# Layer 0 of a two-layer attention backbone: filling products queued behind the score product of three tiles back, and the output projection divided anew over four groups of steps

## The chip, the cores and the metric

The kernel runs on one core of a Trainium2 chip. The metric is the device time of one execution in microseconds, as the median of three runs. A profile of one further execution goes with it. Its engines are named as in the profile: PE is the matrix engine (PEld its loading of the stationary operand), DVE the vector engine, ACT the scalar engine, POOL the general engine, SP the engine that issues most DMA transfers. Each engine works through its own list of instructions in order.

## The reference

Two layers over 1024 latent tokens with a prefix of 256 context tokens, width 1024. The change lies in layer 0, the even layer:

```python
h = rms_norm(x, norm_g[0]) * (1 + scale) + shift          # latent and context tokens
aq, ak, av, ag, bq, bk, bv, bg = split_cols(h @ w_in, EVEN_WIDTHS)
# A: 8 heads on 2 key/value heads, all 1280 keys, RMS norm and rotary on q and k
# B: 8 heads on 2 key/value heads, context keys and a window of +-128, rotary, a sink logit
oa = softmax(q k^T / 8) v ;  ob = the same with window mask and sink
y = concatenate([oa * silu(ag), ob * silu(bg)]) @ w_out
x = x + gate * y                                          # then layer 1, final rms_norm
```

Layer 1 (a convolution module and a neighbourhood attention) follows and isn't touched. Its first step needs the normed rows of layer 0's result.

## The kernel before

All products are made from values split into a high and a low part (`split`, line 310), three matrix products for each (`mm3`, lines 327 to 329): high by high, low by high, high by low. The tokens are cut into chunk 0 (256 context tokens) and chunks 1 and 2 (512 latent tokens each).

**Units.** Layer 0's attention is done in four units, one for each key/value head, in the order 2, 3, 0, 1. Units 2 and 3 are windowed (branch B), units 0 and 1 are global (branch A). A unit has ten blocks of 128 queries, and a block has two to ten tiles of 128 keys: 42 tiles in a windowed unit, 84 in a global one. In this document the tiles of layer 0 are counted through from 0: 0 to 41 and 42 to 83 are the windowed units, 84 to 167 and 168 to 251 the global ones.

**A tile** (`attn_gen`): the score product `st` (line 491, with 495, and 494 for a mask), the exponential on ACT (line 503), the split into `ph` and `pl` (ACT, then POOL or DVE), and three products `ov` (lines 447 to 449) three tiles later. For each block there are also products for the maxima of its scores (`mx`, lines 602, 614, 622), whose results DVE reduces, and a small transpose `trn` (line 425) that puts the maxima into `QL`, which the second half of the score product reads.

**Fill.** Between the tiles stand products of other work: the projection of the next unit (`pq`, `proj_qkv`, 240 products of 384 columns), its gate (`pg`, `proj_gate`, 144 products), and the output projection (`po`, `out0`), in three parts by the units whose results it needs: `out0_part(parts[0])` for the first two units (288 products), `out0_part(parts[1])` for the third (144) and `final_proj` for the fourth (48 for each chunk). `norm_h` makes layer 1's input from a finished chunk. The tails of the projection (`qk_tail`, transposes `trk` at line 858) also stand there. A unit's keys and values lie in one of two buffers in turn.

**What sets the order.** `weave` runs a number of steps of the attention (two for each tile) and draws steps of fill at an even rate between them; `later(FL[0])` gives the fill a lower rank by 80. The finished program's order isn't that of the code: a scheduler takes, for each engine, what is ready by its own reckoning, the attention first by rank. Fill that is ready can so be placed long ahead of the step that drew it. `weave` has an argument `lag`: where it isn't 0, each product of fill is given an edge to the score product that stands `lag` places from the end of the list of those drawn so far (`sts`), and must come behind it in PE's list. Before, layer 1 uses it and layer 0 doesn't.

**Numbers.** `N0` are the steps that the gate's rest is spread over, `NLAST` the steps at a unit's end for which no fill is drawn, `NFILL` the steps of fill drawn between. `O1` are the steps for the output projection in the last unit, by groups: reading back the units' results (`load_oh`), part one, part two, and the share of the final work (`final_proj(1)`, `norm_h(1)`, `final_proj(0)`, `norm_h(0)`) that is drawn before the attention ends. `final_proj(2)` and `norm_h(2)` come behind it all.

Of the kernel before, what the change touches and what calls it, by code (L numbers as in the profile page):

```python
# [67 lines left out]
NFILL = (39, 39, 36)  # L68
GL = 12
HV = 'gggvvvvg'  # L70
O1 = (6, 65, 41, 14)
TICK0, TICK1 = (1, 3)
PLAN = 'p0mmnbwmm1h2nbhnbh'
MWR = "ABxAVx"
# [13 lines left out]
def tile_kernel(ctx: ExitStack, tc: tile.TileContext, a, out):  # L88
# [435 lines left out]
    def weave(main, nmain, fill, nfill, last=True, all_fill=True, lag=0):  # L524

        done = 0
        for k in range(nmain):
            next(main, None)
            while done * nmain < (k + 1) * nfill:
                with ExitStack() as cx:  # L530
                    cx.enter_context(later(FL[layer[0]]))
                    if lag and len(sts) >= lag:
                        cx.enter_context(tc.issue_after(sts[-lag].ins))
                    next(fill, None)
                done += 1
        if all_fill:
            for _ in fill:
                pass
        if last:
            for _ in main:  # L540
                pass
# [131 lines left out]
    with ExitStack() as p0x:  # L673
# [111 lines left out]
        def proj_gate(u, ms):  # L785

            if u not in gw:
                gw[u] = load_g0(u) if u == ORDER[0] else load_w0("ev_g", u)
            wh, wl = gw[u]
            for m, c in ms:  # L790
                t0, n = CHUNKS[c]
                pp = bank("pp", nm("pg"))
                for dk in range(DK):
                    ms_ = slice(m * P, (m + 1) * P)
                    mm3(pp[:, :n], wh[dk][:, ms_], wl[dk][:, ms_], Hs(h, 0, t0, n, dk), Hs(h, 1, t0, n, dk),
                        dk == 0, dk == DK - 1)
                    if dk % 3 == 1:
                        tick()
                        yield
                sg = ap.tile([P, 640], F32, tag="rt2", name=nm("sg"), bufs=2)  # L800
                silu2(pp[:, :n], sg[:, :n])
                mark[0] = SY.dma_start(Gs[u][:, m, t0 : t0 + n], sg[:, :n])
                for _ in range(2):
                    if tails:
                        qk_tail(*tails.pop(0))
# [61 lines left out]
        def gblocks(k):  # L867

            if k == 3:
                blocks = [(m, c) for c in range(3) for m in range(2)]  # L870
                return blocks[:GB], blocks[GB:]
            return [(0, c) for c in range(3)], [(1, c) for c in range(3)]

        def fill0(k, w=None):
            yield from proj_qkv(ORDER[k], w)
            yield from proj_gate(ORDER[k], gblocks(k)[0])
# [4 lines left out]
        main = attn_gen(a0, [group0(u, qb) for u in ORDER for qb in QORD], VS0, LOOK0)  # L881
        for k in range(4):
            u = ORDER[k]
            n = NSTEP[u // 2] + (12 if k == 0 else 0)
            if k < 3:
                n0 = N0[1 + u // 2] if k else N0[0]
                n1 = n - n0 - NLAST[u // 2]
                weave(main, n0, proj_gate(u, gblocks(k)[1]), 9, False)
                weave(main, n1, fill0(k + 1), NFILL[k], False)
                weave(main, NLAST[u // 2], iter(()), 0, False)  # L890
            else:
                weave(main, GL, proj_gate(u, gblocks(k)[1]), 18 - 3 * GB, False)
# [4 lines left out]
    with tc.tile_pool(name="o0", bufs=1, reuse_waits="tile") as op_:  # L897
        U1 = ORDER[-1]
        parts = [[2 * u + k for u in sorted(us) for k in range(2)] for us in (ORDER[:2], ORDER[2:3], ORDER[3:])]
        final = parts[2]  # L900
        x1 = []
        def load_oh(fs):

            f0, f1 = fs[0], fs[-1] + 1
            for c in range(3):
                t0, n = CHUNKS[c]
                if fs == parts[0]:
                    oh[c] = new_h(c)
                    x1.append(op_.tile([P, DK, n], F32, tag=f"x1_{c}", name=nm("x1"), bufs=1))
                for f in range(f0, f1, 2):  # L910
                    lo = oh[c][1][:, f : f + 2, :]
                    (SY, SC)[OHQ].dma_start(lo.bitcast(F32), Od[:, f : f + 2, t0 : t0 + n])
                    split(lo.bitcast(F32), oh[c][0][:, f : f + 2, :], lo, "s", OHE)
                    yield
# [21 lines left out]
        def out0_part(fs):  # L936
            for e2 in range(4):
                w = load_w(op_, a["ev_wo"], e2, 256, WO, dks=fs, rb=2)
                if fs == parts[0]:
                    load_x1(e2)  # L940
                for e in (2 * e2, 2 * e2 + 1):
                    for c in range(3):
                        yield from out0(fs, e, c, *w)
# [30 lines left out]
            yield  # L974

        weave(main, O1[0], load_oh(parts[0]), 6, False)
        weave(main, O1[1], out0_part(parts[0]), 48, False)
        weave(main, O1[2], chain(load_oh(parts[1]), out0_part(parts[1])), 30, False)
        ws = [load_w(op_, a["ev_wo"], e2, 256, WO, "gv"[e2 % 2], dks=final, rb=2) for e2 in range(4)]
        fill = chain(final_proj(1), norm_h(1), final_proj(0), norm_h(0))  # L980
        weave(main, NSTEP[U1 // 2] - GL - O1[0] - O1[1] - O1[2], fill, O1[3])
# [612 lines left out]
```

## Time and profile before

| | |
|---|---|
| three runs, median (lowest to highest) | 1579.01 us (1578.08 to 1581.34) |
| the profiled execution | 1581.59 us |
| its span, first to last instruction | 1579.8 us, 21684 instructions |
| mean clock granted to PE | 0.962 |
| layer 0's attention, first to last score product | 133.0 to 926.5 us |
| windowed units | to 502 us |
| global units | 502 to 926.5 us |

The share of the span is given for each engine; matrix products overlap in the pipeline, so that their busy times are longer than the distance at which they start. Where a row of the trace names a wait, it is the idle time of the engine ahead of an instruction, with what ended it. A row "by stretches" gives a stretch of the span in us, its length, then for each engine busy time and number of instructions, the granted clock, the DMA engines' mean busy share and the rate in GB/s; asked for one line or tile it counts those instructions alone.

### The profile page before, as it was taken

The page shows a single profiled execution, that of the slowest core. Times are in us where ns is not written, and L with a number is a line of the kernel's source. Part 1 is how long each engine was busy: PE and PEld are TensorE (multiplying, and loading weights), DVE is VectorE, ACT ScalarE, POOL GpSimd, SP SyncE. Part 2 cuts the span into 40 slices and gives each one's busy share as a digit, 9 for nine tenths or more (in the row PEclk, how much of TensorE's full clock was granted, in tenths as well). Part 3 has the DMA queues.
Part 4 walks back from the last instruction along what each step waited for, and adds up shares of the span by engine and source line. Part 5 has one row for each costly group of instructions (what it writes and reads, how often), then busy time and mean ns, then how long its engine had stood idle before and what let it go on. Part 6 is the DMA issues. An engine that isn't in the chain of part 4 may idle for free.

```text
span 1579.8 us, 21684 instructions
## 1 busy us (share of the span) xinstructions
PE 1469.3 (93%) x7084; PEld 1172.7 (74%) x7084; DVE 1086.9 (69%) x2279; ACT 748.8 (47%) x1418; POOL 794.1 (50%) x637
## 2 busy tenths in 40 slices
PE   6899999998998999999999879999989999989995
PEld 2785987886886767876766657888877878768874
DVE  2833576588589865566677856999738466787866
ACT  3722333443435555447556654433334355554563
POOL 3531352553445666557556754664532244364665
PEclk8899999998999999999999989999999999979997
DMA  9473324422312253222112022222595577967632
GB/s 367 151 238 127 114 84 153 137 76 90 110 44 82 87 195 129 64 57 62 41 30 88 7 66 77 86 68 72 175 271 194 186 215 218 284 191 231 187 110 107
DMA packets 158105, 208.23 MB, mean 132 GB/s; under 512 B 15068, under 2 KB 96168, under 8 KB 157992
## 3 DMA queue, kind: packets, MB, share of 16 engines
q1 hardware_dynamic: 151328, 195.27, 39.1%
q10 hardware_dynamic: 6664, 11.57, 2.2%
q8 instruction: 56, 0.92, 0.3%
q14 instruction: 57, 0.47, 0.1%
HBM read 152.27 MB, written 53.22 MB: 130 GB/s over the span
## 4 chain that ended last, share of the span: by engine, by line
PE 73%; DVE 15%; DMA 6%; ACT 2%; issue 2%; POOL 1%; SPq 0%; ACTq 0%; DVEq 0%; POOLq 0%
PE p L327 6%; PE p L328 6%; PE p L329 6%; PE ov L447 4%; PE ov L449 4%; PE po L327 4%; PE po L329 4%; PE po L328 4%; PE ov L448 4%; PE st L491 4%; PE st L495 4%; PE pq L327 3%; PE pq L328 3%; PE pq L329 3%; PE pg L329 2%
## 5 line engine op out<-in xcount | busy, mean ns | idle before, releaser
L310 POOL TENSOR_TENSOR pl<-pf,ph 128x512 fp32r<-128x512 f32 (+4 forms) x321 | 392.9, 1235 | 362.8 <-ACT ph L307 280.0
L503 ACT ACTIVATE pf<-st 128x512 f32<-128x512 f32 x284 | 166.0, 596 | 213.7 <-PE st L495 159.2
L310 POOL TENSOR_TENSOR wl<-wr,wh 128x512 fp32r<-128x512 f32 (+2 forms) x131 | 168.7, 1300 | 187.8 <-ACT wh L307 145.9
L307 ACT CAST ph<-pf 128x512 fp32r<-128x512 f32 (+4 forms) x364 | 210.0, 588 | 19.6 <-PE ov L448 9.5
L327 PE MATMUL p<-hh,wh 128*128 128x512 f32 x448 | 180.0, 402 | 11.7 <-ACT wh L307 6.2
L328 PE MATMUL p<-hl,wh 128*128 128x512 f32 x448 | 179.6, 402 | 1.2 <-POOL hl L310 1.2
L329 PE MATMUL p<-hh,wl 128*128 128x512 f32 x448 | 176.3, 399 | 0.0
L491 PE MATMUL st<-QH,KAt 128*128 128x512 f32 (+4 forms) x364 | 142.5, 392 | 7.6 <-DVE pf L500 4.7
L447 PE MATMUL ov<-ph,Vt 128*128 128x512 f32 (+4 forms) x364 | 141.9, 390 | 5.5 <-DVE y L652 3.4
L449 PE MATMUL ov<-pl,Vt 128*128 128x512 f32 (+4 forms) x364 | 142.5, 391 | 4.5 <-POOL pl L310 3.5
L448 PE MATMUL ov<-ph,Vt 128*64 128x512 f32 (+4 forms) x364 | 139.9, 384 | 0.0
L495 PE MATMUL st<-QL,KBt 68*128 68x512 f32 (+4 forms) x364 | 135.8, 386 | 0.0
L307 ACT CAST wh<-wr 128x512 fp32r<-128x512 f32 (+2 forms) x134 | 80.8, 612 | 98.4 <-PE p L328 21.2
L1068 DVE SCALAR_TENSOR_TENSOR cps<-U,taps,cps 128x512 f32<-128x512 f32 x184 | 126.3, 749 | 0.9
L327 PEld LDWEIGHTS p<-hh,wh 128*128 128x128 f32 x448 | 85.4, 191 | 33.0 <-ACT wh L307 7.1
L615 DVE TENSOR_REDUCE mp<-mx 128x1 f32<-128x512 f32 x128 | 85.7, 682 | 25.7 <-PE mx L614 25.2
L328 PEld LDWEIGHTS p<-hl,wh 128*128 128x128 f32 x448 | 85.5, 191 | 21.7 <-POOL hl L310 2.2
L329 PEld LDWEIGHTS p<-hh,wl 128*128 128x128 f32 x448 | 85.3, 190 | 20.6 <-issue 0.5
L449 PEld LDWEIGHTS ov<-pl,Vt 128*128 128x128 f32 x364 | 70.5, 194 | 28.9 <-POOL pl L310 9.9
L327 PE MATMUL pq<-wh,hh 128*128 128x384 f32 x256 | 88.5, 346 | 2.8 <-ACT hh L307 2.8
L491 PEld LDWEIGHTS st<-QH,KAt 128*128 128x128 f32 x364 | 70.0, 192 | 26.3 <-ACT pf L503 6.9
L329 PE MATMUL pq<-wh,hl 128*128 128x384 f32 x256 | 87.4, 341 | 0.0
(277 smaller groups left out, 3482.6 us busy)
## 6 DMA issues: line engine op xcount, KB each, us to landing
mw<-in_mod_w_dram SPq DMA_DIRECT2D x16, 1024.0 KB, 5.7
Q<-qs SPq DMA_DIRECT2D x40, 256.0 KB, 2.1
QH<-Q SPq DMA_DIRECT2D x80, 128.0 KB, 2.7
mw<-in_mod_w_dram SPq DMA_DIRECT2D x16, 512.0 KB, 6.5
wr<-in_od_d_dram SPq DMA_DIRECT2D x32, 256.0 KB, 2.9
wr<-in_ev_qkv_dram SPq DMA_DIRECT2D x16, 384.0 KB, 5.1
KAt<-KD SPq DMA_DIRECT2D x16, 384.0 KB, 5.8
wr<-in_od_wo_dram SPq DMA_DIRECT2D x22, 256.0 KB, 3.3
```

Source lines behind the costliest of these rows:

```text
L307: acts.append(SC.copy(hi, src))
L310: (GP if leng == "g" else VE).tensor_tensor(lo, src, hi.bitcast(F32), op=ALU.subtract)
L327: PE.matmul(o, lh, rh, start=first, stop=False)
L328: PE.matmul(o, lh, rl, start=False, stop=False)
L329: PE.matmul(o, ll, rh, start=False, stop=last)
L447: PE.matmul(o, V[:, 64:192], ph[:, :n], start=(t == 0), stop=False)
L448: PE.matmul(g.ov[0:64, q0 : q0 + n], V[:, 0:64], ph[:, :n], start=False, stop=False)
L449: PE.matmul(o, V[:, 64:192], pl[:, :n], start=False, stop=(last and g.sink is None))
L491: sts.append(PE.matmul(st[:, :n], KA[:, cs], g.QH[:, q0 : q0 + n], start=True, stop=False))
L495: PE.matmul(st[:, :n], KB[0:68, cs], g.QL[0:68, q0 : q0 + n], start=False, stop=True)
L503: acts.append(SC.activation(pf[:, :n], st[:, :n], AF.Exp, scale=1.0 if g.bias else SCALE))
L1068: VE.scalar_tensor_tensor(pc, uc, w, pc, op0=ALU.mult, op1=ALU.add)
```

## The change

Four of layer 0's calls of `weave` get `lag` 3, and three numbers of `O1` are changed. The two calls without fill, the one for the last unit's gate and the last one with the final work don't get it. Nothing that is computed is changed.

```diff
-O1 = (6, 65, 41, 14)
+O1 = (6, 80, 42, 22)
+LAG0 = 3
...
-                weave(main, n0, proj_gate(u, gblocks(k)[1]), 9, False)
-                weave(main, n1, fill0(k + 1), NFILL[k], False)
+                weave(main, n0, proj_gate(u, gblocks(k)[1]), 9, False, True, LAG0)
+                weave(main, n1, fill0(k + 1), NFILL[k], False, True, LAG0)
...
-        weave(main, O1[1], out0_part(parts[0]), 48, False)
-        weave(main, O1[2], chain(load_oh(parts[1]), out0_part(parts[1])), 30, False)
+        weave(main, O1[1], out0_part(parts[0]), 48, False, True, LAG0)
+        weave(main, O1[2], chain(load_oh(parts[1]), out0_part(parts[1])), 30, False, True, LAG0)
```

What it does to the order is seen on PE. In the changed program every line behind the constants has a number that is higher by one. Counted by tiles, the products of fill stand thus:

| | before | changed |
|---|---|---|
| projection of the second unit (240 pq) | tiles 4 to 17 | 4 to 18 |
| of the third | 29 to 47 | 43 to 62 |
| of the fourth | 59 to 85 | 87 to 132 |
| gate of the third (144 pg) | 47 to 59 | 63 to 86 |
| gate of the fourth | 85 to 102 | 133 to 149 |
| output projection, part one (288 po) | 107 to 141 | 175 to 214 |
| part two (144 po) | 141 to 200 | 217 to 235 |
| final work (144 po) | from 217 | from 237 |

Three places on PE show it. The first is tile 31, late in the first windowed unit; `pq` is the projection of the third unit. Before:

```order
L491 MATMUL st_2671<-QH_2225,KAt_540 128x512
L495 MATMUL st_2671<-QL_2226,KBt_538 128x512
L447 MATMUL ov_2683<-ph_2572,Vt_541 128x512
L448 MATMUL ov_2683<-ph_2572,Vt_541 64x512
L329 MATMUL pq_3073<-wh_3055,hc_163 128x384
L327 MATMUL pq_3073<-wh_3055,hc_163 128x384
L328 MATMUL pq_3073<-wl_3056,hc_163 128x384
L329 MATMUL pq_3073<-wh_3055,hc_163 128x384
L327 MATMUL pq_3172<-wh_3049,hc_163 128x384
L449 MATMUL ov_2683<-pl_2573,Vt_541 128x512
```

Changed:

```order
L492 MATMUL st_2671<-QH_2225,KAt_540 128x512
L496 MATMUL st_2671<-QL_2226,KBt_538 128x512
L623 MATMUL mx_2520<-KAt_540,QH_2491 128x384
L448 MATMUL ov_2683<-ph_2572,Vt_541 128x512
L449 MATMUL ov_2683<-ph_2572,Vt_541 64x512
L623 MATMUL mx_2523<-KAt_540,QH_2491 128x384
L450 MATMUL ov_2683<-pl_2573,Vt_541 128x512
```

The projection has left this place; only the attention's own products stand between the scores now.

The second is tile 207, in the last global unit; `po` is part one of the output projection (names `oh` of chunk 1, `hh` and `hl`). Before:

```order
L491 MATMUL st_8251<-QH_7647,KAt_543 128x512
L495 MATMUL st_8251<-QL_7648,KBt_538 128x512
L425 MATMUL trn_8020<-ident,nmt_8017 4x128
L602 MATMUL mx_8113<-KAt_543,QH_8032 128x256 x2
L449 MATMUL ov_8170<-pl_8178,Vt_544 128x512
L447 MATMUL ov_8170<-ph_8206,Vt_544 128x512
L448 MATMUL ov_8170<-ph_8206,Vt_544 64x512
L491 MATMUL st_8269<-QH_7647,KAt_543 128x512
```

Changed:

```order
L492 MATMUL st_8172<-QH_7625,KAt_543 128x512
L496 MATMUL st_8172<-QL_7626,KBt_538 128x512
L448 MATMUL ov_8099<-ph_8135,Vt_544 128x512
L615 MATMUL mx_7959<-KAt_543,QH_7905 128x512
L449 MATMUL ov_8099<-ph_8135,Vt_544 64x512
L330 MATMUL po_8197<-hc_7257,wl_8190 128x256
L328 MATMUL po_8226<-hh_7284,wh_8183 128x512
L329 MATMUL po_8226<-hl_7285,wh_8183 128x512
L330 MATMUL po_8226<-hh_7284,wl_8184 128x512
L328 MATMUL po_8226<-hh_7284,wh_8183 128x512
L492 MATMUL st_8213<-QH_7625,KAt_543 128x512
```

Five products of the output projection stand where there were none.

The third is the end of the attention, behind the last score product; `po` of `hh_7305` is chunk 2, `po` of `hc_7257` chunk 0. Before:

```order
L449 MATMUL ov_9306<-pl_9416,Vt_544 128x512
L447 MATMUL ov_9306<-ph_9438,Vt_544 128x512
L448 MATMUL ov_9306<-ph_9438,Vt_544 64x512
L449 MATMUL ov_9306<-pl_9439,Vt_544 128x512
L327 MATMUL po_9573<-hh_7305,wh_8954 128x512
```

Changed:

```order
L329 MATMUL po_9375<-hc_7257,wh_9075 128x256
L330 MATMUL po_9375<-hc_7257,wl_9076 128x256
L448 MATMUL ov_9349<-ph_9481,Vt_544 128x512
L449 MATMUL ov_9349<-ph_9481,Vt_544 64x512
L328 MATMUL po_9389<-hc_7257,wh_9075 128x256
L329 MATMUL po_9389<-hc_7257,wh_9075 128x256
L330 MATMUL po_9389<-hc_7257,wl_9076 128x256
```

Before, the last products of the attention stand in one piece, with chunk 2's behind them; now 42 of chunk 0's 48 stand between and ahead of chunk 2's. On DVE the twelve operations of chunk 0's `norm_h` stand among chunk 2's eight residual additions (line 933), which before came behind them.

## The prediction

> **What bounds the kernel now.** I read the page's line of busy time first, then busy time by stretches of layer 0, then the same stretches for the score products alone and for each kind of filling product.
>
> ```profile
> PE 1469.3 (93%) x7084; PEld 1172.7 (74%) x7084; DVE 1086.9 (69%) x2279; ACT 748.8 (47%) x1418; POOL 794.1 (50%) x637
> ```
>
> No engine but PE is near full. The next rows are the stretches (length, then busy us and instructions of PE, PEld, DVE, ACT, POOL, the granted clock, DMA): 133 to 502 is the windowed units, 502 to 927 the global units, 927 to 966 the end of layer 0.
>
> ```profile
> 133.00:476.00 343.00, 330.13 (x1750) 281.11 (x1749) 241.03 (x638) 134.25 (x289) 144.64 (x110) 0.98 0.31 101
> 476.00:502.00 26.00, 22.46 (x91) 13.98 (x89) 22.92 (x56) 15.04 (x32) 16.26 (x13) 1.00 0.24 71
> 502.00:600.00 98.00, 91.44 (x441) 71.90 (x442) 72.57 (x142) 52.83 (x102) 62.89 (x46) 1.00 0.45 153
> 600.00:698.00 98.00, 98.00 (x478) 79.63 (x477) 55.53 (x102) 45.07 (x77) 54.24 (x42) 1.00 0.24 70
> 698.00:749.00 51.00, 49.06 (x202) 34.53 (x201) 36.26 (x67) 36.90 (x62) 37.81 (x30) 0.97 0.19 53
> 749.00:807.00 58.00, 57.48 (x275) 46.08 (x274) 37.76 (x68) 31.77 (x54) 33.30 (x26) 1.00 0.14 40
> 807.00:865.00 58.00, 52.76 (x219) 38.88 (x217) 46.78 (x87) 36.24 (x65) 34.38 (x28) 0.94 0.19 65
> 865.00:927.00 62.00, 50.91 (x219) 36.67 (x218) 49.84 (x90) 43.09 (x84) 42.77 (x37) 0.89 0.03 9
> 927.00:966.00 39.00, 31.50 (x132) 24.49 (x131) 16.55 (x30) 12.56 (x22) 12.44 (x11) 0.91 0.32 103
> ```
>
> PE is full from 600 to 698 and from 749 to 807. In the other stretches it waits, and these are not DMA stretches. The score products (line 491, one a tile) in the same stretches:
>
> ```profile
> 133.00:476.00 343.00, 29.10 (x73) 13.52 (x71) 0.98 0.31 101
> 476.00:502.00 26.00, 5.11 (x13) 2.26 (x12) 1.00 0.24 71
> 502.00:600.00 98.00, 11.87 (x29) 5.45 (x29) 1.00 0.45 153
> 600.00:698.00 98.00, 12.60 (x32) 6.02 (x32) 1.00 0.24 70
> 698.00:749.00 51.00, 12.48 (x32) 6.16 (x32) 0.97 0.19 53
> 749.00:807.00 58.00, 9.16 (x24) 4.33 (x23) 1.00 0.14 40
> 807.00:865.00 58.00, 11.27 (x27) 5.32 (x27) 0.94 0.19 65
> 865.00:927.00 62.00, 11.14 (x24) 5.07 (x24) 0.89 0.03 9
> ```
>
> The filling products: pq (two rows), pg (two rows), po (five rows).
>
> ```profile
> 133.00:476.00 343.00, 135.10 (x672) 118.28 (x672) 12.46 (x26) 0.98 0.31 101
> 502.00:600.00 98.00, 8.82 (x48) 8.23 (x48) 1.82 (x4) 1.00 0.45 153
> 133.00:476.00 343.00, 80.32 (x360) 62.47 (x360) 10.32 (x17) 9.15 (x17) 0.98 0.31 101
> 502.00:600.00 98.00, 33.09 (x144) 24.17 (x144) 3.57 (x6) 3.15 (x6) 1.00 0.45 153
> 502.00:600.00 98.00, 5.65 (x28) 4.51 (x29) 1.23 (x2) 1.00 0.45 153
> 600.00:698.00 98.00, 60.98 (x273) 46.74 (x271) 15.73 (x24) 1.00 0.24 70
> 749.00:807.00 58.00, 28.67 (x131) 22.42 (x132) 13.79 (x21) 1.00 0.14 40
> 807.00:865.00 58.00, 13.01 (x51) 9.05 (x49) 5.98 (x8) 0.94 0.19 65
> 865.00:927.00 62.00, 8.58 (x48) 7.54 (x48) 4.40 (x9) 0.89 0.03 9
> ```
>
> What one product costs in a full queue is the distance of starts, not its length:
>
> ```profile
> 200.94 0.33 PE L327 MATMUL pq<-wh,hh 128*128 128x384 f32 x1
> 201.46 0.34 PE L327 MATMUL pq<-wh,hh 128*128 128x384 f32 x1
> 588.96 0.28 PE L327 MATMUL po<-hc,wh 128*128 128x256 f32 x1
> 589.31 0.28 PE L327 MATMUL po<-hc,wh 128*128 128x256 f32 x1
> 946.24 0.40 PE L327 MATMUL po<-hh,wh 128*128 128x512 f32 x1
> 946.94 0.39 PE L327 MATMUL po<-hh,wh 128*128 128x512 f32 x1
> ```
>
> Three products lie between the rows of each pair: 0.173 us for 384 columns, 0.117 for 256, 0.233 for 512. A pg or po is of 512 columns twice for once of 256, 0.194 on average; from 807 to 865 all are of 512, from 865 to 927 of 256. So the fill takes 116 + 70 = 186 us of 133 to 476, 8 + 28 + 5 = 41 of 502 to 600, then 53, 0, 25, 12 and 6. What is left, by tile:
>
> - windowed: (343 - 186) / 73 = 2.15 us with fill, 26 / 13 = 2.00 without any.
> - global: 57 / 29 = 1.97, 45 / 32 = 1.41 (full PE), 51 / 32 = 1.59 (no fill), 33 / 24 = 1.38 (full PE), 46 / 27 = 1.70, 56 / 24 = 2.33; all together 288 us for 168 tiles, 1.71.
>
> A global tile thus costs 1.4 us where fill lies evenly between tiles, 1.6 where there is none, and 1.7 to 2.3 where fill comes in lumps with special waits. The windowed tiles aren't helped by fill: DVE is busy 22.92 of 26 us there.
>
> **The change, part by part.** It adds and removes no computation; on PE it adds only an order. By the order of both programs the projection of the third unit (240 pq) moves from tiles 29 to 47 to tiles 43 to 62, that of the fourth from 59 to 85 to 87 to 132, and the first part of the output projection from 107 to 141 to 175 to 214. Some 43 us of fill leave the windowed units for the global ones. Before, 300 po stand in tiles 87 to 150, 12 in 202 to 217, 78 in 218 to 237; now 0, 102 and 138. Without fill stay tiles 151 to 175, as before 146 to 177; tiles 28 to 40 lose theirs (37 us to 2), tiles 68 to 83 keep little.
>
> Global units, by tiles now, against 288 us:
> - 84 to 150, 67 tiles, projections spread: between 1.41 and 1.97. Their kind of fill stood in the 1.97 stretch, whose row has gates and DVE work too; their even spread is that of the 1.41 stretch. I take 1.65: 111 us.
> - 151 to 175, 25 tiles without fill at 1.59: 40 us.
> - 176 to 237, 62 tiles with 84 us of fill, evenly: between 1.38 and 1.70. Nearest is 749 to 807, the same products in the same unit; with a few waits kept, 1.48: 92 us.
> - 238 to 251, 14 tiles, with the final projections and the norm of chunk 1 squeezed into them. Between 1.41 and 2.33; DVE work is the same (49.84 of 62 us), so 2.2: 31 us.
>
> Sum 274, a gain of 14 us.
>
> Windowed units: 13 tiles lose fill and go from 2.15 to 2.00 or stay, nothing of note. Two long waits there can go:
>
> ```profile
> PE mx L622 <- DVE mp L623: 3.7, 1, 3.7
> 383.28 0.87 PE L858 MATMUL trk<-ident,pc 128*128 128x128 f32 x3 [3.70 <-DVE KAt L310]
> 387.66 0.63 PE L328 MATMUL pg<-hl,wh 128*128 128x512 f32 x1
> 388.09 0.63 PE L329 MATMUL pg<-hh,wl 128*128 128x512 f32 x1
> ```
>
> The first row is of the waits (total, times, longest). They come where the tails of projections run ahead into DVE's queue, which holds the maxima. After the second, products of 0.63 us start 0.43 apart, not 0.233, until 391.5: (391.5 - 387.2) x 0.2 / 0.43 = 2 us more. So both are worth 3.7 + 3.7 + 2 = 9 us at most. The projection of unit 0 still runs under unit 3, so other such waits may come; between +4 and -9 I take -6.
>
> The end: 42 of the 48 products of chunk 0 (5 us, conserved, they leave the tiles above) now stand between and behind the last ov products, where PE waited:
>
> ```profile
> 935.03 2.08 PE L327 MATMUL po<-hh,wh 128*128 128x512 f32 x4 [3.51 <-ACT hh L307]
> ```
>
> The wait of 3.51 us for the last y stays, since those 42 stand ahead of it. DVE gets the 12 operations of chunk 0's norm among the residual additions of chunk 2, and the products after those need the norm of chunk 2. An addition over 512 columns took 5.98 / 8 = 0.75 us (the po row of 807 to 865, DVE's column), so over 256 some 0.4, and twelve 5 us; PE's remaining products cover part. Between -3 and +8 I take +3; the 42 products themselves cost nothing here, since they have left the tiles ahead.
>
> Queues: the added edges hold back PE alone. DMA issues of weights (SP) move with their products, and DMA is at 3 to 45% in these stretches, so I cost them nothing; without that cover a set of weights would be late as in the second rival.
>
> Sum: -14 - 6 + 3 = **-17**, say -18 with less time at a low clock. Against the profiled execution's 1581.6 us this is 1563.6; the runs' median is 1579.0, 2.6 below it, so 1561.
>
> [...] By matmul busy time the global units hold 425 - 399.7 = 25 us at most; by weight loads at the 0.81 of the full stretch, 425 - 307.7 / 0.81 = 45 us. [...]
>
> **The rivals.**
> - *Much more.* All filled global tiles go at 1.41 and the 14 last at 1.7: 67 x 1.41 + 40 + 62 x 1.38 + 24 = 244, a gain of 44; with -6 and +3, 1532. For it: 600 to 698 held this for 98 us. Against: the pieces of a projection bring DVE and ACT work that po does not.
> - *Slower: weights turn over too late.* A set of weights can be split only when the products of the set before have left its buffers, and a lagged product can't be put elsewhere while it waits: PE stands, the tile's attention behind it.
>
> ```profile
> PE po L327 <- ACT wh L307: 1.5, 1, 1.5
> L310 POOL TENSOR_TENSOR wl<-wr,wh 128x512 fp32r<-128x512 f32 (+1 forms) x34 | 49.0, 1449 | 48.6 <-ACT wh L307 48.6
> ```
>
>  Some ten sets follow from tile 84 on. With a wait of 1.5 us and one subtraction of 1.45 us each, 10 x 3 = 30 us: 1591. It decides from six sets on. Against: one such wait in 660 us now.
> - *The waits only move.* Tiles without fill are still 25 global and about 29 windowed; if the filled ones keep 1.71, the sum is -6 + 3: 1576, to 1580 without the windowed gain. An edge that doesn't bind would give the same, but the order shows that it binds.
> - *The clock.* If the stretches without fill brought waits of 3 us and more, each costs 2 us again. Tiles 28 to 40 and 68 to 83 hold six group changes: 6 x 5.7 = 34 us, 1595. [...]
>
> **How the numbers follow.** Forecast (1550 to 1573) 0.58, much more 0.12, waits only move (1573 to 1582) 0.14, slower by weights 0.11 or clock 0.05. A measurement of this kernel tells about 0.2%, 3 us, from no change. So faster 0.74, same 0.10, slower 0.16. The range leaves out the far half of the first rival and the outer part of the slow ones: 1538 to 1583.
>
> **What would show it.** Rest by tile of 1.5 from tile 176 to 237, and no stretch of 2 us a tile before 238; PE full there as from 600 to 698; tiles 151 to 175 still at 1.6; the two waits of 3.7 us gone; the norm of chunk 2 some us later after the last score. Wrong if po waits for wh or wl at each set, if tiles 84 to 150 stay near 2.0, or if the windowed units, with 43 us of fill less, don't end about 45 to 50 us earlier.

## The result: slower by 2.2%, and the profile after

The changed kernel takes 1613.61 us (median of 4 runs, 1611.94 to 1616.95), the kernel before, beside it, 1580.04 us (1578.08 to 1581.34): a ratio of 1.022, with a 95% interval of 1.0205 to 1.0234. The profiled execution took 1611.94 us, its span 1610.2 us; the forecast was 1561 us, so that it was wrong in sign. Mean clock 0.964 (before 0.962); in the other three runs it was 0.957 to 0.961.

The page's line of busy time of the changed kernel hardly differs from that of before, so that the work is the same:

```profile
PE 1479.1 (92%) x7084; PEld 1174.4 (73%) x7084; DVE 1079.5 (67%) x2279; ACT 748.1 (46%) x1418; POOL 795.0 (49%) x637
```

The next two views are busy time by stretches (start and end, length, then busy us and instructions of PE, PEld, DVE, ACT, POOL, the clock, DMA), cut at the same tiles in both kernels: the windowed units, tiles 84 to 150, 151 to 175, 176 to 237, 238 to 251, and from the last score product to layer 1's first product. Before:

```profile
133.00:502.00 369.00, 352.59 (x1839) 295.10 (x1837) 263.95 (x693) 149.29 (x319) 160.90 (x123) 0.98 0.31 99
502.00:705.00 203.00, 196.44 (x950) 156.83 (x951) 132.05 (x252) 102.56 (x187) 122.00 (x91) 1.00 0.34 109
705.00:748.00 43.00, 41.06 (x165) 28.48 (x165) 32.08 (x60) 32.18 (x54) 31.95 (x25) 0.96 0.17 46
748.00:898.00 150.00, 138.03 (x622) 106.12 (x621) 116.03 (x207) 89.52 (x159) 91.67 (x71) 0.95 0.14 46
898.00:927.00 29.00, 24.11 (x93) 16.26 (x91) 18.58 (x38) 21.63 (x44) 19.79 (x20) 0.88 0.02 5
927.00:949.00 22.00, 17.27 (x59) 12.66 (x59) 10.97 (x18) 8.86 (x16) 10.87 (x9) 0.84 0.43 138
```

Changed:

```profile
131.00:476.00 345.00, 318.13 (x1594) 253.31 (x1594) 237.67 (x634) 139.86 (x298) 143.81 (x112) 0.98 0.31 99
476.00:679.00 203.00, 188.84 (x898) 154.92 (x897) 135.28 (x286) 103.31 (x195) 120.70 (x89) 0.97 0.23 72
679.00:730.00 51.00, 44.02 (x182) 29.16 (x181) 38.66 (x69) 34.70 (x58) 39.77 (x30) 1.00 0.61 205
730.00:902.00 172.00, 169.68 (x812) 136.40 (x811) 101.79 (x192) 84.16 (x145) 89.11 (x69) 1.00 0.13 38
902.00:937.00 35.00, 31.19 (x136) 23.60 (x135) 22.18 (x35) 20.34 (x36) 20.66 (x17) 0.95 0.16 60
937.00:973.00 36.00, 24.44 (x110) 18.41 (x109) 28.70 (x53) 20.95 (x45) 21.00 (x20) 0.91 0.27 88
```

The filling products of the changed kernel in these stretches, pq (two rows), pg (two), po (three):

```profile
131.00:476.00 345.00, 99.23 (x480) 85.68 (x480) 9.63 (x20) 0.98 0.31 99
476.00:679.00 203.00, 54.23 (x240) 45.83 (x240) 4.78 (x10) 0.97 0.23 72
131.00:476.00 345.00, 67.85 (x317) 52.85 (x318) 8.75 (x15) 7.92 (x15) 0.98 0.31 99
476.00:679.00 203.00, 43.38 (x188) 32.57 (x186) 5.34 (x9) 4.23 (x8) 0.97 0.23 72
730.00:902.00 172.00, 99.97 (x425) 74.23 (x426) 31.33 (x48) 1.00 0.13 38
902.00:937.00 35.00, 13.02 (x50) 9.34 (x49) 5.98 (x8) 0.95 0.16 60
937.00:973.00 36.00, 20.98 (x90) 15.56 (x90) 8.86 (x15) 0.91 0.27 88
```

At the prediction's prices (0.173 us a pq, 0.194 a pg or po on average) the fill is 480 x 0.173 + 317 x 0.194 = 145 us in the windowed units, 78 in tiles 84 to 150, 2 in 151 to 175, 83 in 176 to 237, 10 in 238 to 251, and 42 x 0.117 + 48 x 0.233 = 16 behind. What is left is the rest, in us:

| stretch | rest before | rest forecast | rest changed |
|---|---|---|---|
| windowed units | 369 - 186 = 183 | 177 | 345 - 145 = 200 |
| tiles 84 to 150 | 203 - 94 = 109 | 111 | 203 - 78 = 125 |
| 151 to 175 | 43 | 40 | 51 - 2 = 49 |
| 176 to 237 | 150 - 42 = 108 | 92 | 172 - 83 = 89 |
| 238 to 251 | 28 | 31 | 35 - 10 = 25 |
| last score to layer 1's first product | 22 - 11 = 11 | 14 | 36 - 16 = 20 |

So the windowed units lost 17 us, the global tiles gained 19 + 3 and gave back 16 + 6, and the end lost 9: 26 us, less 2 for the earlier first score. Another 6 lie behind layer 1's first product (637 us to the end against 631): no line of layer 1 is changed, but the scheduler's order there differs in places. Where these 6 arise was not traced.

Where PE waited shows in the waits up to the last score product (who waits, for whom, us in total, times, longest). Changed, the four rows with the most:

```profile
PE mx L603 <- DVE QL L427: 13.2, 10, 2.5
PE trn L426 <- DVE nmt L422: 12.7, 5, 7.9
PE st L492 <- ACT pf L504: 7.0, 13, 1.5
PE ov L448 <- DVE y L653: 4.8, 8, 1.3
```

Before, the same two kinds were:

```profile
PE trn L425 <- DVE nmt L421: 3.7, 3, 2.8
PE mx L602 <- DVE QL L426: 2.0, 3, 1.1
PE trn L425 <- DVE nmt L415: 1.9, 3, 0.9
```

These belong to one chain, the **maxima's chain**: DVE reduces a block's maxima to `nmt`, PE transposes them (`trn`), DVE reads that into `QL`, and then the second half of the block's first score product can go. With another 1.6 us of `nmt` rows it is 27.5 us in the changed kernel, 7.6 before. (The expectations below give 30.4 and 8.9, counted in another way.) The longest one, in the changed kernel's trace of PE (start, length, instruction, in brackets the idle time ahead of it):

```profile
390.76 0.38 PE L426 MATMUL trn<-ident,nmt 128*12 128x128 f32 x1 [7.94 <-DVE nmt L422]
390.86 0.77 PE L603 MATMUL mx<-KAt,QH 128*128 128x256 f32 x2
392.20 0.80 PE L603 MATMUL mx<-KAt,QH 128*128 128x256 f32 x2 [0.58 <-DVE QL L427]
392.80 1.05 PE L496 MATMUL st<-QL,KBt 68*128 68x512 f32 x2
395.05 0.63 PE L495 MATMUL st<-bmt,ident 128*128 128x512 f32 x1
395.47 0.63 PE L496 MATMUL st<-QL,KBt 68*128 68x512 f32 x1
```

The same block's `trn` (tile 59) before:

```profile
418.99 0.39 PE L328 MATMUL pg<-hl,wh 128*128 128x512 f32 x1
419.22 0.27 PE L425 MATMUL trn<-ident,nmt 128*12 128x128 f32 x1
```

`trn` stands ahead of the block's own `st` second half, and of the next block's `mx`. Before, 9.3 us of filling products (at the prediction's prices) stood between the last score product ahead of it and `trn`, which didn't wait; now it is 3.5 us, and PE stood 7.94 us. After it, products start 0.42 us apart (395.05, 395.47) instead of 0.233. The wait on `QL` has a second root: `trn` takes one of the two PSUM banks of the maxima (`bank("mx", ...)`, line 424), so the next block's `mx` can't start until DVE has read it.

At the end, where before one wait of 3.51 us stood, PE now waits several times, most often for DVE's residual additions `x`; three of the rows:

```profile
943.45 0.39 PE L328 MATMUL po<-hc,wh 128*128 128x256 f32 x1 [1.67 <-DVE x L934]
946.31 0.38 PE L328 MATMUL po<-hc,wh 128*128 128x256 f32 x1 [0.18 <-DVE x L934]
952.93 1.22 PE L328 MATMUL po<-hh,wh 128*128 128x512 f32 x2 [4.26 <-ACT hh L308]
```

Chunk 0's products wait for additions, and chunk 2's, which wait for `hh` as before, stand behind them.

### The profile page after: what moved, and what is told of

It reads as the page before. It is cut to its first block, busy times and chain, and to the rows that moved or that the text cites. A ratio compares the mean times of both kernels' runs of the same rounds, so it can differ in the third digit from the quotient of the medians.

```text
span 1610.2 us, 21657 instructions
## 1 busy us (share of the span) xinstructions
PE 1479.1 (92%) x7084; PEld 1174.4 (73%) x7084; DVE 1079.5 (67%) x2279; ACT 748.1 (46%) x1418; POOL 795.0 (49%) x637
## 5 line engine op out<-in xcount | busy, mean ns | idle before, releaser
L329 PE MATMUL pq<-wl,hh 128*128 128x384 f32 x256 | 88.6, 346 | 0.0
```

What stands on the lines that cost most here:

```text
L329: PE.matmul(o, lh, rl, start=False, stop=False)
```

## The experiments

All ratios are to the kernel before on the same chip, with 95% intervals. The table gives, from the traces, the start of tile 84, of the last score product and of layer 1's first product, and the waits on the maxima's chain (`nmt` and `QL` rows) up to the last score product, all in us.

| kernel | tile 84 | last score | layer 1 | chain | time, ratio |
|---|---|---|---|---|---|
| before | 501 | 927 | 949 | 7.6 | |
| changed | 476 | 937 | 973 | 27.5 | 1613.61, 1.022 |
| e1 | 481 | 955 | 975 | 28.0 | 1610.42, 1.0193 (1.0176 to 1.021) |
| e2 | 500 | 924 | 961 | 10.4 | 1593.48, 1.0084 (1.0069 to 1.0099) |
| e3 | 501 | 926 | 950 | 8.9 | 1586.14, 1.0041 (1.0026 to 1.0056) |
| e4 | 478 | 948 | 970 | 27.7 | 1611.28, 1.0204 (1.0186 to 1.0223) |
| e5 | 489 | 953 | 974 | 23.9 | 1606.30, 1.0178 (1.0163 to 1.0193) |
| e6 | 499 | 949 | 970 | 17.3 | 1607.64, 1.0187 (1.0172 to 1.0202) |
| e7 | 466 | 908 | 930 | 2.9 | 1562.91, 0.9901 (0.9886 to 0.9916) |
| e8 | 459 | 902 | 945 | 0.2 | 1581.31, 1.0005 (0.9987 to 1.0023) |
| e9 | 493 | 953 | 975 | 22.6 | 1616.90, 1.0229 (1.0205 to 1.0252) |
| e10 | 475 | 946 | 965 | 18.2 | 1598.20, 1.0118 (1.009 to 1.0146) |
| e11 | 509 | 957 | 977 | 18.1 | 1601.28, 1.0128 (1.0108 to 1.0148) |
| e12 | 501 | 934 | 957 | 8.8 | 1591.18, 1.0069 (1.0049 to 1.0089) |
| e13 | 487 | 919 | 945 | 10.9 | 1578.65, 0.9992 (0.9981 to 1.0004) |
| e14 | 477 | 918 | 965 | 4.3 | 1600.38, 1.014 (1.0125 to 1.0155) |
| e15 | 460 | 912 | 937 | 0.2 | 1567.68, 0.9938 (0.9917 to 0.996) |
| e16 | 478 | 925 | 953 | 5.5 | 1584.75, 1.0033 (1.0018 to 1.0048) |
| e17 | 476 | 933 | 961 | 4.3 | 1592.47, 1.0085 (1.0068 to 1.0101) |

### Which call costs: e1 to e4

e1, the lag on the projections and the gate alone:

```diff
-                weave(main, n0, proj_gate(u, gblocks(k)[1]), 9, False)
-                weave(main, n1, fill0(k + 1), NFILL[k], False)
+                weave(main, n0, proj_gate(u, gblocks(k)[1]), 9, False, True, 3)
+                weave(main, n1, fill0(k + 1), NFILL[k], False, True, 3)
```

> The lag of 3 on the two calls for projection and gate alone; the output projection as before. Theory A (the projections are at fault: held back, they leave tiles without fill and put DVE's tails of the projection beside the maxima): most of the loss of 33 us appears here, 1600 to 1615 us, with windowed tiles (to tile 83) that wait some 19 us more than before, and tiles 84 to 150 some 16 us more. Theory B (the output projection, held back and squeezed into the last tiles, is at fault): 1575 to 1585 us here.

e2, the lag on the output projection's two calls, with the new O1:

```diff
-O1 = (6, 65, 41, 14)
+O1 = (6, 80, 42, 22)
...
-        weave(main, O1[1], out0_part(parts[0]), 48, False)
-        weave(main, O1[2], chain(load_oh(parts[1]), out0_part(parts[1])), 30, False)
+        weave(main, O1[1], out0_part(parts[0]), 48, False, True, 3)
+        weave(main, O1[2], chain(load_oh(parts[1]), out0_part(parts[1])), 30, False, True, 3)
```

> The lag of 3 on the two calls for the output projection, with the new O1; projections as before. Theory A: tiles 176 to 251 gain some 18 us, tiles 103 to 175 lose their fill (35 tiles from 1.4 to 1.6 us, 7 us), the end behind the last score costs some 9 to 14 us more: 1575 to 1585 us. Theory B: nearly the whole loss, 1600 to 1615 us.

e3 is e2 with O1 as before, and e4 is e1 and e3 together:

```diff
-O1 = (6, 80, 42, 22)
+O1 = (6, 65, 41, 14)
```

> As the run before with the old O1, (6, 65, 41, 14): 48 output products behind the last score product, as in the kernel before, where the new O1 has 90. Theory A with the end's cost put down to the new last group: 10 to 14 us below the run before, 1564 to 1574 us, first projection of layer 1 some 22 us behind the last score. If the end's cost comes from the lag and not from O1, the same time as the run before.

> The lag on all four calls, the old O1. Theory A: the changed kernel without the end's 10 to 14 us, 1600 to 1604 us. If the new O1 costs nothing: 1613 us.

The projections' lag alone loses 31 us, nearly all of the change's 33.6. The output's lag loses 6.4 by itself (e3): the gain from tile 176 on, which was forecast, is there, but tiles 107 to 150, left bare of fill, cost as much. The new O1 costs 7.3 more beside that lag (e2 against e3, less than expected) and 2.3 beside all of them (changed against e4, where the two intervals overlap): it moves work from the tiles to the end. Of these four, e1 fell in A's range; e2 (between the ranges of A and B), e3 (12 us above its range) and e4 (near its second value, 1613) missed A's.

### Longer lags: e5 and e6

Lag 12 and lag 30 in place of 3 on the projections and the gate:

```diff
-                weave(main, n1, fill0(k + 1), NFILL[k], False, True, 3)
+                weave(main, n1, fill0(k + 1), NFILL[k], False, True, 12)
```

> The lag on projection and gate alone, but 12 tiles in place of 3. Theory C (fill is worth most where a block of queries changes and the score waits for its maxima, and the lag takes it from there): by the order, fill of 92 us stands in those waits of the windowed units, with a lag of 3 it is 83 and with none 113; so some 21 / 30 of the loss of 31 us stays, 1597 to 1604 us. Theory E (what hurts is only the length of the gaps without fill, tiles 28 to 40): this order's gap is shorter by 9 tiles, so half of the loss or less, 1585 to 1592.

> The same with a lag of 30 tiles. The windowed units have nearly the order of before (104 us of fill in the waits; the third projection at tiles 29 to 47 as before), and only the fourth projection moves, from tiles 59 to 85 to 60 to 104. Theory C: 9 / 30 of the loss, 1585 to 1592 us. If the loss came from the fourth projection running under the global units: 1595 us or more.

Both missed what theory C expected: e6 leaves the windowed units nearly as they were (tile 84 at 499) and still loses 28 us. Its waits on the chain fall to 17.3, but other waits come up: 10.2 us for `y` (before 3.4) and 7.7 for `pf` (2.7), summed over their rows. How far fill is held back isn't what decides.

e6's other expectation, 1595 us or more if the fourth unit's projection costs by running under the global units, holds by its number; but e13 below has that projection there too and loses nothing in the whole. The clock isn't ruled out as a part: the mean granted clock was 0.949 to 0.952 in the eight runs of e5 and e6 and 0.953 to 0.955 in e1's, against medians of 0.961 and 0.963 in the runs of before beside them. Worked out from these means, that is 14 to 17 us of full clock, an estimate of the most that it can have cost. In the changed kernel (median 0.961) it is at most a few us, and e13 has 0.953 to 0.960 without a loss. No run tests it apart.

### The chain cut: e7 and e8

In layer 0 `trn` reads a constant, so that no PE instruction waits for a block's maxima (they are still computed); e8 is the changed kernel with the same cut. These kernels leave the maxima out of the scores, so they don't compute the reference's result.

```diff
+    nmc = cp.tile([P, 12], F32R, tag="nmc", name="nmc")
+    VE.memset(nmc.bitcast(F32), 0.0)
...
-        PE.transpose(tr2[0:nr, 0:P], nmt[:, 0:nr].bitcast(F32), ident)
+        PE.transpose(tr2[0:nr, 0:P], (nmt if layer[0] else nmc)[:, 0:nr].bitcast(F32), ident)
...
-                acts.append(SC.activation(pf[:, :n], st[:, :n], AF.Exp, scale=1.0 if g.bias else SCALE))
+                acts.append(SC.activation(pf[:, :n], st[:, :n], AF.Exp, scale=1.0 if g.bias else 0.01))
```

> The kernel before, with the scores' dependence on their maxima cut in layer 0: the small transpose reads a constant zero in place of the negated maxima, and the exponential is scaled by 0.01 so that it stays finite. All products, reductions and transposes are still done, but no score waits for a reduction of its own block. Both theories: faster than before, 1530 to 1570 us.

> The changed kernel with the same cut (constant zero for the negated maxima in layer 0, exponential scaled by 0.01). Theory C: the loss of 33 us falls to that of the end, at most 12 us over the run before. Theory D (DVE's work bounds the windowed units, waits or not, so that fill moved out of them costs its whole length elsewhere): DVE has the same work, and 20 us or more over the run before stay.

By its time alone e8 speaks against C: 18 us over e7, between the two expectations. By stages it speaks for it: e8 reaches its last score product 6 us *ahead* of e7 (902, 908), where the changed kernel comes 10 us behind before (937, 927). All of e8's loss lies behind that, 43 us from there to layer 1 against 22. So two things were mixed, and they had to be taken apart.

### Fill in the waits, or fill in the windowed units: e9 to e12

e9 draws the lagged projections only in a block's last two tiles, so that lumps stand at the changes of block again (its core, in `weave` and `attn_gen`):

```diff
+            chg[0] = t >= len(g.tiles) - 2
...
-            while done * nmain < (k + 1) * nfill:
+            while done * nmain < (k + 1) * nfill and (not lag or chg[0]):
```

> The kernel before, with the projections and the gate issued behind the lagged score product as in e1, but drawn only in the last two tiles of each block of queries, so that a lump of them stands where the next block's first scores wait for its maxima. By the order of issue 105 us of filling products then stand between the two halves of a block's first score in the windowed units (113 before, 83 in e1), while the third projection still lies in tiles 90 to 136, as in e1 (87 to 132; before 59 to 85). Theory C (the lag takes away the products that covered the wait for the maxima): most of e1's loss comes back, 1583 to 1595 us, and PE's idle time ended by the maxima's chain falls from 31 us to 15 or less. Theory D (what costs is that the products leave the windowed units, where VectorE sets the pace and PE has time to spare, for the global units, where PE is full): nothing comes back, 1603 to 1615 us.

e10 puts the lag on the third projection alone, e11 on the first two:

```diff
-                weave(main, n1, fill0(k + 1), NFILL[k], False)
+                weave(main, n1, fill0(k + 1), NFILL[k], False, True, 3 if k == 2 else 0)
```

> The kernel before, with the lag on the third projection and its gate alone (the first two stay in tiles 4 to 29 and 29 to 59 as before; the third goes from 59 to 85 into tiles 87 to 131). Filling products in the waits of the windowed units: 81 us by the order of issue (113 before, 83 in e1). Theory D: this is the part of e1 that moves work from the windowed to the global units, so nearly all of e1's loss, 1603 to 1612 us. Theory C, with the loss spread over the blocks that lose their cover (10 windowed blocks bare of fill): also a loss, but by the waits alone (about 10 windowed blocks at 1.5 us more, and the global ones as in e1), 1590 to 1602 us.

> The kernel before, with the lag on the first two projections and their gates alone. The second projection goes from tiles 29 to 47 into 43 to 62, the third is pushed from 59 to 85 into 75 to 87, so that the products stay in the windowed units, but smoother: 101 us in the waits (113 before, 83 in e1), nothing changes from tile 105 on. Theory D: the units keep their products, 1576 to 1584 us. Theory C: tiles 28 to 42 and 62 to 74 are bare, a loss of a third to a half of e1's, 1588 to 1597 us.

e12 is e3 with a lag of 45 in place of 3:

```diff
-        weave(main, O1[1], out0_part(parts[0]), 48, False, True, 3)
+        weave(main, O1[1], out0_part(parts[0]), 48, False, True, 45)
```

> The kernel before, with a lag of 45 score products on the output projection's calls, old O1. Its products then lie in tiles 133 to 167 and 167 to 195 (before 107 to 141 and 141 to 200; with a lag of 3, in e3, 175 to 211), and the tail is as before. In e3 tiles 176 to 251 came out 26 us faster and tiles 107 to 150, left bare, 23 us slower beside their fill. If fill is worth the same wherever it lies among the global tiles: 1576 to 1584 us. If the bare stretch 107 to 132 costs as in e3 by the tile (0.52 us, 13 us) and the gain is only on the tiles that now have fill and had none (151 to 175, about 0.3 us each): 1584 to 1590 us.

These decide little. e9 got nothing back and lies just above D's range: the chain's waits fell only to 22.6, so a count of products that stand in a wait by the order of issue doesn't tell how long PE waits there. e10 falls in C's range, e11 (21 us lost though its products stay in the windowed units) outside both and far from D's, e12 just above its second expectation. e10 and e11 lose 18 and 21 us; together more than e1's 31.

### The chain loosened: e13 and e14, and cut without the tail: e15

e13 lets `trn` take the PSUM bank of the other transposes in layer 0; nothing is left out. e14 is the changed kernel with the same edit.

```diff
-        tr2 = bank("mx", nm("trn"))
+        tr2 = bank("mx" if layer[0] else "tr", nm("trn"))
```

> The kernel before; in layer 0 the small transpose of a block's maxima takes the PSUM bank of the other transposes instead of one of the two banks of the maxima, so that a block's maxima needn't wait until VectorE has read the transpose of the block ahead. Nothing is left out. By the order of issue the transpose then stands between the halves of its block's first score in 9 of 20 windowed blocks (before 16) and 1 of 20 global ones (5), and the projections come out spread without any lag: the third in tiles 78 to 129 (before 59 to 85), the output's first part in 159 to 201 (107 to 141). Theory C (the chain through the maxima's banks is what lumps of products had covered; where it is loose, even products cost nothing): PE's idle time ended by the maxima's chain 4 us or less (before 8.9), 1560 to 1576 us. Theory D (products that leave the windowed units cost, whatever the waits): as e10, 1590 to 1605 us.

> The changed kernel with the same other bank for the small transpose. Theory C: most of the 21 us more that PE idles behind the maxima's chain in the changed kernel (30.4 against 8.9) comes back, 1587 to 1600 us. Theory D: the placement of the products is that of the changed kernel (third projection in tiles 91 to 133, changed 87 to 132), so nothing comes back, 1605 to 1618 us.

e15 is e7 with e1's edit:

> e7 (layer 0's transpose reads a constant instead of the maxima, with a smaller scale in the exponential; the output isn't the reference's) with the lag of 3 on the projections and the gate alone; the tail is that of before. In the full program this lag cost 31 us (e1). Theory C: without the wait for the maxima it costs 0 to 10 us over e7's 1563: 1560 to 1573 us. Theory D: it costs nearly all of the 31 here too, 1583 to 1596 us.

In the sum this answers what the projections' lag costs. In e15 it costs 5 to 6 us over e7 (4.8 by the medians, 0.37% of 1580 by the ratios), where it cost 31 with the chain in place; D's range lay 15 us and more above. e14 gets 13 us back, and its largest waits on the chain, by the same view as above, are

```profile
PE st L495 <- DVE QL L426: 1.3, 3, 0.8
PE trn L425 <- DVE QL L426: 1.1, 1, 1.1
```

4.3 us in all. e14 reaches its last score product at 918 us, 8 ahead of before.

By stages it answers only the global tiles. e14's windowed units, then its tiles 84 to 150:

```profile
132.00:477.00 345.00, 320.57 (x1599) 257.69 (x1598) 231.28 (x641) 142.88 (x297) 144.65 (x112) 0.96 0.31 98
477.00:667.00 190.00, 181.98 (x888) 149.01 (x888) 132.05 (x282) 104.36 (x194) 122.02 (x90) 1.00 0.24 75
```

Tiles 84 to 150 have 78 us of fill as in the changed kernel, and their rest falls from 125 to 112 us: the chain's waits there fall from 8.5 to 0.7 us, and the clock rises from 0.97 to 1.00. The windowed units have 143 us of fill, and their rest, 345 - 143 = 202, is that of the changed kernel (200), though the chain's waits there fell from 16.1 to 3.6. All of PE's waits in these units are 24 us (changed 27, before 15.5): others took the chain's place, among them 9.6 us (changed 2.6) for DVE's reads of the projection's transposes `trk`, with which `trn` now shares a bank,

```profile
PE trk L858 <- DVE KAt L310: 5.2, 2, 3.6
PE trn L425 <- DVE KAt L310: 4.4, 2, 2.4
```

and the clock there is 0.96 against 0.98, worth some 7 us at most by these two figures. With the chain cut, the windowed units of e7 and then e15 are

```profile
133.00:466.00 333.00, 326.26 (x1705) 271.23 (x1704) 247.17 (x640) 146.24 (x307) 153.96 (x117) 0.99 0.35 109
133.00:460.00 327.00, 316.32 (x1599) 255.24 (x1598) 239.76 (x636) 142.58 (x298) 145.75 (x112) 0.98 0.33 104
```

with 164 and 145 us of fill: 19 us of fill leave for 6 us of time, and the rest rises from 169 to 182.

e13 shows the same order without a lag: its scheduler puts the third projection (that of the fourth unit) in tiles 78 to 129, nearly where the changed kernel has it, and in the whole it costs nothing: 0.9992. By stages it is an exchange: the rest of its windowed units is 355 - 159 = 196 (before 183), and that of tiles 176 to 237, where the output's first part now lies, 160 - 72 = 88 (before 108). A clock of 0.95 in its windowed units (before 0.98) may be up to 11 of the 13 us there. It missed C's range by 3 us all the same, and its chain waits, expected at 4 or less, were 10.9, among them one of 3.6 us of another transpose that shares the new bank.

### The end: e16 and e17

e16 is e14 with the output projection's calls and O1 as before; e17 is e14 with other numbers:

```diff
-O1 = (6, 80, 42, 22)
+O1 = (6, 50, 30, 14)
```

> e14 (the changed kernel with the other bank for the small transpose) with the lag on the projections and the gate alone and the output projection and O1 as before: 48 products of the output projection behind the last score product instead of 96. In e14's profile the last score product stood at 918 us, 9 ahead of before's, but layer 1's first product came 47 us behind it, where before had 22. If the rest of e14's loss is this end: 1570 to 1580 us. If the lag costs beside it: 1590 to 1600.

> e14 with O1 = (6, 50, 30, 14): the lag stays on all four calls, but the output projection's first two parts take 80 steps instead of 122, so that the final work starts at tile 230 (e14 241) and 48 products stand behind the last score product (e14 96). If the order of the end is what e14 loses: the stretch from the last score product to layer 1's first product falls from 47 to 22 to 28 us, 1575 to 1585 us. If the lag itself holds up the end: 1592 to 1602 us.

The stretch from the last score product to layer 1's first product, e14 first and then e17:

```profile
918.00:965.00 47.00, 30.18 (x134) 23.82 (x132) 30.67 (x61) 23.46 (x49) 22.78 (x22) 0.82 0.21 69
933.00:961.00 28.00, 18.37 (x68) 13.54 (x67) 17.16 (x35) 14.15 (x30) 15.77 (x15) 0.82 0.32 111
```

In e17 the end falls from 47 to 28 us, as expected, but the tiles ahead of it take 14 us more, since the 48 products now stand there: 8 us of median come back, not the 15 to 25 expected, and the time, 1592.47, lies at the edge of the other expectation's range. A long end is mostly work that has moved. e16 shows the projections' lag once more with a loose chain: 1584.75, 6 us over e13 (6.5 by the ratios), whose own order is already spread. The plainer comparison is with e1, which has the same lag and the old bank: 5 us over before (1.0033) instead of 31 (1.0193). Of that gain 11 us of rest lie in tiles 84 to 150 (123 and 112) and 13 in tiles 176 to 237 (104 and 91), 2 in the windowed units (204 and 202). e16 missed its range by 5 us. The output's lag with the new O1 costs the other 16 (e14 over e16).

No version that computes the reference's result beat the kernel before; e13 equals it.

## Why the prediction was wrong, step by step

- **"The windowed tiles aren't helped by fill" failed**, and with it "13 tiles lose fill ... nothing of note" (forecast for these units: -6 us, measured +17). 2.00 us for a bare tile was read from one stretch of 26 us. Fill of 41 us left, and the time fell by 24: 17 of the 41 had cost nothing there. In the changed kernel's trace the chain's waits in these units are 12 us longer (16.1, before 4.2), and at tile 59 the trace shows fill gone and a wait come. By the order of issue `trn` stands between the halves of its block's first score in 16 of 20 windowed blocks, before and after; before, 113 us of fill stand there with it, now 83. But e9, which puts 105 us there, gets nothing back, and the chain isn't shown to be the cause in these units: loosened (e14, e16) it leaves their rest at 202, and cut (e15 over e7) it still lets 19 us of fill leave for 6 us of time. What hides the fill there stays open: DVE's load (busy 240 of 327 us in e15, 238 of 345 in the changed kernel) was not tested apart.
- **"84 to 150 at 1.65" and "151 to 175 at 1.59" were too low**: 125 / 67 = 1.87 and 49 / 25 = 1.96 us, in all 23 us. The even spread was to bring the 1.41 of the full stretch, but the same 67 tiles had had 109 / 67 = 1.63 already. The condition "wrong if tiles 84 to 150 stay near 2.0" came true. In tiles 84 to 150 the cause is shown to be the chain, with the clock that went with it: loosened (e14, e16), the rest is 112 us, near the 111 forecast, and cut it is 115 (e15) and 111 (e7). In tiles 151 to 175 it isn't: the chain's waits there are 1.3 us, and with the chain cut (e8) these tiles take 58 us with 5 of fill. That stays open.
- **"176 to 237 at 1.48" was right**: 89 / 62 = 1.44, PE 169.68 busy of 172. 238 to 251 came out at 25 / 14 = 1.8, better than the 2.2 taken.
- **The two waits of 3.7 us** are gone, as said, but not as a gain: the changed kernel has one of 7.94 us instead, and the chain waits 20 us more. The rival "the waits only move" had this mechanism, at a price of nothing; the rival "the clock" counted six changes of block among tiles left bare, 34 us, and came nearest (1595), though it charged them to the clock, whose mean hardly moved in this kernel (0.957 to 0.964 in its four runs, 0.962 in the profile of before).
- **The end, +3**, was mis-sized: +9 of rest, and 36 us against 22 in length. "They cost nothing here, since they have left the tiles ahead" is half right: e17 shows the exchange, e2 against e3 that it isn't even.
- **Weights too late** didn't come: no wait of `po` for `wh` is among the large ones.
- The order of issue was read rightly (tile 84 came 25 us earlier; 45 to 50 was the sign asked for, and its absence the first hint), and PE did become full where the forecast had it. What was missing was what each lump stood *in front of*, and what its products cost in the stretch that they left.

What stays open: why lags of 12 and 30, and bursts at the changes of block, bring back so little. In the first two the wait for `y` comes up (12.7 and 10.2 us) as that of the chain falls, in the third it hardly does (4.6), and each has another order on DVE and a lower mean clock than the runs of before beside it (e5 and e6 0.949 to 0.952 against 0.960 to 0.967, e9 0.953 to 0.962 against 0.960 to 0.965); no run here isolates that. The parts of e1's loss don't add up from e10 and e11 either.

## What to carry to other kernels

Before smoothing work that a scheduler has put in lumps, look at what stands behind each lump in the engine's list: a lump may be the cover of a wait on another engine, and the trace shows no wait there just because it is covered (at tile 59, 9.3 us of fill and no wait before, 3.5 us and a wait of 7.94 us after). Judge fill by how much the time of a stretch falls when fill leaves it, over several bare stretches, not by one. Loosen the chain first (here: a bank that two blocks shared), then spread; here that took away most of what the projections' lag had cost (e16) and brought no gain. And compare two kernels by stage, since a loss at the end can hide a gain ahead of it.

## What the runs showed of the chip that was not expected

PE's list in the windowed units is the same, instruction for instruction, in the changed kernel and in e1, and both have the same two short waits there. Changed, then e1 (start, length, instruction, idle time ahead):

```profile
260.64 0.44 PE L623 MATMUL mx<-KAt,QH 128*128 128x384 f32 x1 [1.11 <-DVE mp L624]
262.77 0.87 PE L859 MATMUL trk<-ident,pc 128*128 128x128 f32 x3 [1.69 <-DVE KAt L311]
```

```profile
261.29 0.45 PE L622 MATMUL mx<-KAt,QH 128*128 128x384 f32 x1 [1.12 <-DVE mp L623]
263.41 0.87 PE L858 MATMUL trk<-ident,pc 128*128 128x128 f32 x3 [1.68 <-DVE KAt L310]
```

Behind them the clock (the third number from the end) went apart. Changed, then e1, by stretches of 10 us:

```profile
260.00:270.00 10.00, 5.98 (x22) 3.93 (x23) 8.40 (x30) 2.33 (x8) 0.00 (x0) 0.83 0.40 139
270.00:280.00 10.00, 8.68 (x37) 5.54 (x37) 9.05 (x21) 5.28 (x10) 6.41 (x5) 1.00 0.22 69
280.00:290.00 10.00, 8.11 (x36) 5.60 (x35) 8.69 (x26) 5.84 (x11) 5.08 (x4) 1.00 0.23 66
```

```profile
260.00:270.00 10.00, 6.52 (x20) 4.37 (x20) 7.95 (x28) 1.37 (x5) 0.04 (x1) 0.65 0.39 131
270.00:280.00 10.00, 10.00 (x32) 7.17 (x31) 7.41 (x19) 6.02 (x11) 6.30 (x5) 0.67 0.25 79
280.00:290.00 10.00, 7.94 (x24) 5.35 (x24) 8.16 (x23) 4.73 (x9) 4.23 (x4) 0.67 0.08 24
```

So no single wait above 1.7 us stands just ahead of the low clock in either, only these two with one product between, and what followed differs between two executions of one order: about 1.7 us of full clock lost in one, 10 in the other over 30 us, worked out from the clock of these rows. The prediction's rival "the clock" counted waits of 3 us and more alone; no run here shows such a bound. For the reading of a single profile of this kernel the two executions mean that differences of some 5 us in one stage may be the clock's: with this same list the windowed units took 345 us in the changed kernel and 350 in e1, and from 263 to 330 us the clock was 0.98 in the one and 0.82 in the other.
